# Two hybrid-encoder layers on one core: the linear attention's values leave the PE transposes and travel through device memory, the output projection starts in two banks of another pool, and a pool closes two tiles later

## The chip, the cores and the metric

The kernel runs on one core of a Trainium2 chip. The metric is the device time of one execution in microseconds, as the median of several runs; smaller is better. Before the change it is 2322.85 us (three runs, 2322.03 to 2323.6).

## What is computed

Two encoder layers run over 272 positions (16 learned meta tokens and 256 grid tokens) of width 2048, in float32. Each layer makes one combined projection, runs two groups of heads beside each other on its columns, joins them by an output projection, and follows with two post-LN steps and a squared-ReLU MLP:

```python
proj = jnp.einsum('bld,dp->blp', h, w_in)
gq, gk, gv, gr, glr, nq, nk, nv = jnp.split(proj, points, axis=-1)
y_gla = _gla_mixer(gq, gk, gv, gr, glr, gla_w_up, gla_b_up, gla_norm_w)   # 4 heads, dk 128, dv 256
y_na = _na_mixer(nq, nk, nv, na_rel_bias)                                 # 16 heads of 64
mix = jnp.einsum('blm,md->bld', jnp.concatenate([y_gla, y_na], axis=-1), w_out)
h = _layer_norm(DEEPNORM_ALPHA * h + mix, ln1_w, ln1_b)
ff = jnp.einsum('blf,fd->bld', jnp.square(jax.nn.relu(jnp.einsum('bld,df->blf', h, w_ff1))), w_ff2)
return _layer_norm(DEEPNORM_ALPHA * h + ff, ln2_w, ln2_b)
```

The GLA heads (gated linear attention, both directions) need each position's values v as rows: positions on the partitions, the 256 value channels along them. Their output is normalised per head by `rsqrt(mean(o*o))`, so a sum over 256 channels is needed per position. The NA heads (neighbourhood attention) are softmaxes over a window of keys plus the 16 meta tokens; in the first layer the meta tokens' own softmax is computed too. The last layer needs only the 256 grid tokens behind its attention.

## The kernel before

**Matmuls.** Every float32 product is made of three: each operand is split into a high part (rounded to the matmul's type, fp32r) and a low part, the rest, and high x high, high x low and low x high are summed in PSUM. Weights stream in by SP's DMA as `raw` tiles of 128 x 1024. ACT casts each to `wh` (L218) and DVE subtracts to get `wl` (L219); the rings of `raw`, `wh` and `wl` are three deep, and the weight tile behind the one in use is asked for ahead. One weight tile feeds 24 matmuls of 128 x 272.

**Two ways through a projection.** `by_m` (L317) makes one output tile (128 columns of the projection by 272 positions) at a time, in one PSUM bank of the pool `pm` (tiles called "mm", four banks), over the whole depth of 2048. `by_k` (L279) makes four output tiles at once, each in a bank of its own, two blocks of the depth at a time: it can begin while later parts of its input are still being made. The pool `pb` (tiles called "bg", four banks, `bank()`) holds what the background work needs.

**Background.** Attention, gates and normalisation are Python generators in two queues, `fg` and `bg`. Between weight tiles `pump` (L127) steps them, so that their instructions fall among the projection's matmuls. Every engine runs its own instructions in the order in which it got them, so an instruction that waits holds back all behind it on its engine.

**A layer** (L353 on). The columns of the projection come in this order. First k and the values of heads 0 and 1, by `by_k` (in layer 0 eight tiles, four of them in banks of `pb`; in layer 1 the values alone). Then the values of heads 2 and 3 by `by_m`, four tiles; then q. Meanwhile the gates are made (L470 to L494: a low-rank product, its copy `lrt`, the cast `lr` on ACT, and matmuls that read `lr`). Then the gate r and the 24 tiles of the NA heads' q, k and v, in six groups of four; beside these the four GLA heads run as `gla_head` in `bg`. Before the last group (`g == 5`) all of `bg` is forced out, the pool of the GLA heads is closed (`gctx.close`) and that of the layer norm opened (`ln_open`). Then `by_k` makes the first four tiles of the output projection `w_out` (L413), reading `self.y`, which the last NA pair is still filling: `mixed` waits block by block for what is done. Its other twelve tiles go by `by_m`.

**Values.** The projection leaves v with channels on the partitions. `ev_v` (L503) copies a result tile to `ft` on ACT; when a head's two tiles are there, `v_rows` (L510) turns them with six PE transposes (L518: two 128 x 128 and one of 16 columns for each tile) into two "mm" banks, from which ACT casts the high part `V` (L339), DVE subtracts the low part (L340, into `vlow`, which lies in tiles of `y` that are not used yet), and `stack` (L345, L346) places the 16 meta rows in `VS`.

**Other lines of the change.** In `gla_head`, L721 squares the two halves of a head's output on ACT (`grs`, `gtn`), L725 adds them on DVE, L339 and L340 split the sum (`sp`), and `mean` (L976) sums it over the channels by matmuls with a matrix of constants (L983). In an NA pair, `softmax` (L752) runs on the scores `ns` and, in layer 0, on the meta rows' scores `nms`; its reciprocals are on DVE (L757), the multiplies by them (L760) on POOL for `ns` and `npr` and on DVE for `nms`. DVE then turns `ns` and `npr` in squares of 32 x 32 (L799, L800) and ACT's queue sends the result to device memory as `hop` (L819), whence SP's queue fetches it in four pieces (L826); that puts keys on the partitions. PE turns the pair's values and, in layer 0, `nms` (L805, L806, L808) into a "bg" bank.

Of the kernel before, what the change touches and what calls it, by code (L numbers as in the profile page):

```python
# [14 lines left out]
P = 128  # L15
# [24 lines left out]
PITCH = 288  # L40
WIDE = 1280
# [17 lines left out]
class Trunk:  # L59
# [219 lines left out]
    def by_k(self, acts, n, before, wide=False):  # L279

        ps = [self.pm.tile([P, 512], F32, name="mm", tag="mm") for _ in range(4)]
# [3 lines left out]
        for k in range(0, nk, 2):  # L285
# [4 lines left out]
            for g in range(0, len(ps), 4):  # L290
# [62 lines left out]
    def layer(self, l):  # L353
# [4 lines left out]
        with ExitStack() as actx:  # L358
# [8 lines left out]
            self.V = a.tile([P, 2 * GH, 2, P], F32R, name="V", tag="V")  # L367
# [3 lines left out]
            self.y, self.gate, self.done, self.vt = [None] * DC, {}, set(), []  # L371
# [7 lines left out]
            with ExitStack() as ectx:  # L379
# [11 lines left out]
                self.credit, self.alone = 0, True  # L391
                self.by_m(self.x, [L] * 4, lambda m, ps: self.ev_v(4 + m, ps), pump=(1, 1, True))
# [3 lines left out]
            with ExitStack() as gctx:  # L396
# [106 lines left out]
    def ev_v(self, c, ps):  # L503
        vt = self.ep.tile([P, L], F32, name="ft", tag="ft", bufs=4)
        self.nc.scalar.copy(vt, ps)
# [4 lines left out]
    def v_rows(self, h, vt):  # L510

        nc = self.nc
        yield True
        pt = self.spare(2)
        for i in range(3):
            n = P if i < 2 else NM
            for e in range(2):
                nc.tensor.transpose(pt[e][:n, i * P:i * P + P], vt[e][:, i * P:i * P + n], self.ident)  # L518
        for e in range(2):
            self.split(pt[e][:, :T], self.V[:, 2 * h + e].rearrange("p i c -> p (i c)"), self.vlow[h][:, e * T:e * T + T])  # L520
# [761 lines left out]
```

## Time and profile before

| | |
|---|---|
| median of three runs | 2322.85 us |
| the profiled execution | 2323.91 us, its span 2322.1 us |
| clock granted to TensorE | 0.999 |
| PE busy | 2304.2 us (99%), 18420 matmuls |
| DVE busy | 1526.4 us (66%) |
| ACT busy | 1223.0 us (53%) |
| POOL busy | 155.4 us (7%) |
| DMA | 431.65 MB, mean 186 GB/s |

The profile's page gives, for one execution, the busy time of each engine; the chain of waits (the work that ended last, followed back through whatever released it); groups of instructions by line; and the DMA queues. A row of a timeline shows the start, the duration, the engine, the line, the operation, what it writes and reads ("out<-in"), the shape, how many such instructions follow each other, and in square brackets how long the engine stood idle ahead of it and for whom. Lines are those of the kernel before unless said otherwise.

### The profile page before, as it was taken

What the parts mean: (1) busy time and instruction counts of PE and PEld (TensorE: products, weight loads), DVE (VectorE), ACT (ScalarE), POOL (GpSimd) and SP (SyncE); (2) the same over time, 40 slices, a digit from 0 to 9 for tenths busy, and PEclk for the clock granted to TensorE, in tenths of its full rate; (3) what the DMA queues carried; (4) which work ended last, traced back from release to release, by engine and by line L of the source; (5) the groups of instructions that cost most, each with busy time, mean ns of one, the idle gap of its engine ahead of it and who ended that gap; (6) DMA issues with size and microseconds to landing.
All of it is one profiled execution on the core that took longest, in us unless ns stands there. A gap on an engine that the chain in (4) does not pass through costs nothing.

```text
span 2322.1 us, 45272 instructions
## 1 busy us (share of the span) xinstructions
PE 2304.2 (99%) x18420; PEld 2188.9 (94%) x18420; DVE 1526.4 (66%) x2408; ACT 1223.0 (53%) x2096; POOL 155.4 (7%) x232
## 2 busy tenths in 40 slices
PE   9999999999999999999999999999999999999998
PEld 9999999999999999999999899889988888888888
DVE  5588878875544455547576788688866555666655
ACT  5666655564433344444456766655654334555443
POOL 0023210100000000000020122200100000000000
PEclk9999999999999999999999999999999999999999
DMA  8556666565555556665655556665666666667664
GB/s 259 155 164 184 199 189 177 173 181 181 182 181 178 179 181 182 180 179 178 182 173 173 173 175 209 195 187 181 198 191 196 194 191 193 192 196 218 195 195 150
DMA packets 129824, 431.65 MB, mean 186 GB/s; under 512 B 14792, under 2 KB 23496, under 8 KB 129616
## 3 DMA queue, kind: packets, MB, share of 16 engines
q1 hardware_dynamic: 127024, 421.95, 59.9%
q10 hardware_dynamic: 2592, 6.82, 0.8%
q8 instruction: 144, 2.36, 0.4%
q14 instruction: 64, 0.52, 0.1%
HBM read 420.32 MB, written 8.39 MB: 185 GB/s over the span
## 4 chain that ended last, share of the span: by engine, by line
PE 91%; DVE 5%; ACT 2%; issue 1%; DMA 1%; POOL 0%; DVEq 0%; ACTq 0%; SPq 0%
PE mm L253 53%; PE mm L265 29%; PE mm L304 4%; PE mm L314 2%; DVE wl L219 1%; PE bg L304 1%; ACT wh L218 1%; ACT ns L756 0%; DVE S L615 0%; PE bg L851 0%; PE bg L470 0%; PE bg L629 0%; DVE acc L1085 0%; POOL dec L617 0%; DMA raw<-in_wff 0%
## 5 line engine op out<-in xcount | busy, mean ns | idle before, releaser
L219 DVE TENSOR_TENSOR wl<-raw,wh 128x1024 fp32r<-128x1024 f32 (+1 forms) x770 | 935.9, 1223 | 621.8 <-ACT wh L218 518.5
L218 ACT CAST wh<-raw 128x1024 fp32r<-128x1024 f32 (+1 forms) x770 | 804.7, 1047 | 755.8 <-PE mm L253 352.6
L253 PE MATMUL mm<-x,wh 128*128 128x272 f32 (+3 forms) x4544 | 806.8, 294 | 0.0
L253 PEld LDWEIGHTS mm<-x,wh 128*128 128x128 f32 x4544 | 648.0, 188 | 15.5 <-issue 0.8
L253 PE MATMUL mm<-x,wl 128*128 128x272 f32 (+3 forms) x2432 | 520.6, 285 | 2.9 <-DVE wl L219 2.9
L253 PEld LDWEIGHTS mm<-x,wl 128*128 128x128 f32 x2432 | 391.4, 188 | 3.4 <-DVE wl L219 3.4
L253 PE MATMUL mm<-y,wh 128*128 128x272 f32 (+1 forms) x1440 | 235.0, 285 | 0.0
L253 PEld LDWEIGHTS mm<-y,wh 128*128 128x128 f32 x1440 | 199.7, 188 | 0.1
L265 PE MATMUL mm<-x,wh 128*128 128x512 f32 x832 | 193.8, 390 | 0.0
L265 PEld LDWEIGHTS mm<-x,wh 128*128 128x128 f32 x832 | 154.3, 188 | 31.0
L253 PE MATMUL mm<-u,wh 128*128 128x272 f32 (+1 forms) x1056 | 172.1, 285 | 0.0
L265 PE MATMUL mm<-y,wh 128*128 128x512 f32 x688 | 162.3, 389 | 0.0
L265 PEld LDWEIGHTS mm<-y,wh 128*128 128x128 f32 x688 | 128.7, 188 | 26.8 <-issue 0.4
L253 PE MATMUL mm<-y,wl 128*128 128x272 f32 (+1 forms) x720 | 146.5, 284 | 0.0
L253 PEld LDWEIGHTS mm<-u,wh 128*128 128x128 f32 x1056 | 146.3, 188 | 0.0
L265 PE MATMUL mm<-u,wh 128*128 128x512 f32 x496 | 118.3, 391 | 0.0
L253 PEld LDWEIGHTS mm<-y,wl 128*128 128x128 f32 x720 | 112.5, 188 | 0.0
L265 PEld LDWEIGHTS mm<-u,wh 128*128 128x128 f32 x496 | 90.9, 188 | 17.6
L253 PE MATMUL mm<-u,wl 128*128 128x272 f32 (+1 forms) x528 | 107.4, 284 | 0.0
L265 PEld LDWEIGHTS mm<-x,wl 128*128 128x128 f32 x832 | 98.5, 188 | 2.1
L265 PE MATMUL mm<-x,wl 128*128 128x256 f32 x832 | 99.0, 276 | 0.0
L265 PEld LDWEIGHTS mm<-y,wl 128*128 128x128 f32 x688 | 84.3, 188 | 2.8
(275 smaller groups left out, 2285.0 us busy)
## 6 DMA issues: line engine op xcount, KB each, us to landing
raw<-in_wff SPq DMA_DIRECT2D x512, 512.0 KB, 3.6
raw<-in_win SPq DMA_DIRECT2D x190, 512.0 KB, 4.2
raw<-in_wout SPq DMA_DIRECT2D x64, 512.0 KB, 3.9
hop<-nt ACTq DMA_DIRECT2D x16, 384.0 KB, 2.3
np<-hop SPq DMA_DIRECT2D x64, 96.0 KB, 4.1
nb<-in_nab SPq DMA_DIRECT2D x16, 352.0 KB, 4.4
xraw<-in_xT SPq DMA_DIRECT2D x7, 272.0 KB, 5.8
out<-out SPq DMA_DIRECT2D x5, 256.0 KB, 3.1
```

Source lines behind the costliest of these rows:

```text
L218: self.nc.scalar.copy(h, r)
L219: self.wl = self.nc.vector.tensor_tensor(lo, r, h.bitcast(F32), ALU.subtract).ins
L253: mm(o, lhsT=self.block(w, j), rhs=rhs, start=first and not i, stop=last and i == len(TURNS[once]) - 1)
L265: self.nc.tensor.matmul(o, lhsT=self.block(both[j // 8][low], j % 8), rhs=rhs, start=first and not i + j, stop=bool(last and i and j == 15 ...
L304: self.nc.tensor.matmul(ps[g + m][:, :n], lhsT=self.block(parts[p][0], 4 * j + m if first else 2 * m + j), rhs=acts[k + j][parts[p][1]][:, ...
L314: self.nc.tensor.matmul(o, lhsT=self.block(both[low], i), rhs=rhs, start=not low and k + i % 2 == 0, stop=k == DC - 2 and i % 2 == 1 and n ...
```

## The change

Five edits:

1. `by_k` for `w_out` takes its first two result tiles from `pb` and only the last two from `pm` (`ends=True`), and orders the matmuls of the first weight tile by result tile too, the "bg" tiles first.
2. The last NA group is run as two halves of two tiles. Forcing out `bg`, closing the GLA pool and opening the layer norm's come between the halves, two tiles later than before.
3. The values: `ev_v` copies to a tile `ft` padded to 128 x 288 (DVE zeroes the last 16 columns) and turns it in 32 x 32 squares on DVE. A generator `v_flow` then moves each head: `w` writes the turned tile to device memory (`vhop`, 295 KB), `r` reads it back in eight pieces of 32 partitions (32 KB each, straight into `vlow`) and one of 16 (`vm`, the meta rows), all on POOL's DMA queue; `s` casts `V` from what landed (ACT, 128 x 512), subtracts the low part in place (DVE) and stacks the meta rows. The columns of v in the weights are permuted beforehand to fit. The PE transposes and their two "mm" banks go.
4. The sum of the two squared halves (L725) moves from DVE to POOL.
5. The multiply of the meta rows' softmax (L760 for `nms`) moves from DVE to POOL.

```diff
-    def by_k(self, acts, n, before, wide=False):
-        ps = [self.pm.tile([P, 512], F32, name="mm", tag="mm") for _ in range(4)]
+    def by_k(self, acts, n, before, wide=False, ends=False):
+        tile = lambda n: [self.pm.tile([P, 512], F32, name="mm", tag="mm") for _ in range(n)]
+        ps = [self.bank(), self.bank()] + tile(2) if ends else tile(4)
...
-                    order.sort(key=lambda o: (k and o[2], o[1] // 2, o[2]))
+                    order.sort(key=lambda o: ((k or ends) and o[2], o[1] // 2, o[2]))
...
                 for g in range(6):
-                    if g == 5:
-                        while self.bg:
-                            self.step(self.bg, 1)
-                        gctx.close()
-                        self.ln_open()
                     ns = [n if (4 * g + m) % 3 == 0 else L for m in range(4)]
-                    self.by_m(self.x, ns, lambda m, ps: self.ev_na(4 * g + m, ps), pump=(1, GLA_NA, True))
+                    for at in ((0, 2), (2, 4)) if g == 5 else ((0, 4),):
+                        if at == (2, 4):
+                            while self.bg:
+                                self.step(self.bg, 1)
+                            gctx.close()
+                            self.ln_open()
+                        self.by_m(self.x, ns[slice(*at)], lambda m, ps: self.ev_na(4 * g + at[0] + m, ps), pump=(1, GLA_NA, True))
             self.alone = False
-            ps = self.by_k(self.y, n, self.mixed)
+            ps = self.by_k(self.y, n, self.mixed, ends=True)
...
     def ev_v(self, c, ps):
-        vt = self.ep.tile([P, L], F32, name="ft", tag="ft", bufs=4)
-        self.nc.scalar.copy(vt, ps)
-        self.vt.append(vt)
-        if c % 2:
-            (self.fg if c > 3 else self.bg).append(self.v_rows(c // 2, self.vt[-2:]))
+        e = c % 2
+        if not e:
+            self.vt = self.ep.tile([P, VR, 2, 32], F32, name="vt", tag="vt", bufs=4)
+        t = self.ep.tile([P, VR * 32], F32, name="ft", tag="ft", bufs=2)
+        self.nc.scalar.copy(t[:, :L], ps)
+        self.nc.vector.memset(t[:, L:], 0.0)
+        self.nc.vector.transpose(self.vt[:, :, e, :], t)
+        if e:
+            self.vts.append(self.vt)
...
+    def v_flow(self):
+        nc, ep = self.nc, self.ep
+        hops, metas = {}, {}
+        def w(h):
+            hops[h] = self.hp.tile([P, VR, 64], F32, name="vhop", tag="vhop", bufs=4)
+            nc.gpsimd.dma_start(hops[h], self.vts[h].rearrange("p j e c -> p j (e c)"))
+        def r(h):
+            raw = self.vlow[h][:, :2 * T].bitcast(F32).rearrange("p (i a c) -> p i a c", i=2, a=4)
+            metas[h] = ep.tile([NM, GDV], F32, name="vm", tag="vm", bufs=4)
+            at = hops[h].rearrange("(a k) j c -> k j a c", a=4)
+            for j in range(VR - 1):
+                nc.gpsimd.dma_start(raw[j % 4 * 32:j % 4 * 32 + 32, j // 4], at[:, j])
+            nc.gpsimd.dma_start(metas[h].rearrange("p (a c) -> p a c", a=4), at[:NM, VR - 1])
+        def s(h):
+            low, to = self.vlow[h][:, :2 * T], self.VS[:, h * GDV:h * GDV + GDV]
+            high = self.V[:, h].rearrange("p i c -> p (i c)")
+            nc.scalar.copy(high, low.bitcast(F32))
+            nc.vector.tensor_tensor(low, low.bitcast(F32), high.bitcast(F32), ALU.subtract)
+            self.stack(metas[h], to, NM, (0, 32), 64)
+        for f, h in ((w, 0), (w, 1), (r, 0), (w, 2), (r, 1), (s, 0), (r, 2), (w, 3), (s, 1), (r, 3), (s, 2), (s, 3)):
+            while len(self.vts) <= h:
+                yield
+            f(h)
+            yield
...
-        nc.vector.tensor_tensor(rs, rs, tn, ALU.add)
+        nc.gpsimd.tensor_tensor(rs, rs, tn, ALU.add)
...
-            self.softmax(sm, mt, 2, ((sm, sm),), nc.vector)
+            self.softmax(sm, mt, 2, ((sm, sm),), nc.gpsimd)
```

The rows below are instructions in the order in which each engine gets them: the line, the operation, what it writes and reads, the shape, and "x2" where two alike follow each other. Names are those of the tiles; the numbers behind a name only tell tiles apart. The lines of the changed kernel stand a little further down than those of before (L218 and L219 become L219 and L220, L304 becomes L306).

**ACT, the value stage of layer 0**, from the last casts ahead of the gates on. Before:

```order
L218 CAST wh<-raw 128x1024 x2
L475 COPY lrt<-bg 32x272
L505 COPY ft<-mm 128x272
L339 CAST V<-mm 128x256
L345 CAST lr<-lrt 32x272 x2
L345 CAST VS<-mm 16x128 x2
L339 CAST V<-mm 128x256
L345 CAST VS<-mm 16x128 x2
L218 CAST wh<-raw 128x1024
```

and now:

```order
L219 CAST wh<-raw 128x1024 x2
L512 COPY ft<-mm 128x272
L479 COPY lrt<-bg 32x272
L347 CAST lr<-lrt 32x272 x2
L538 CAST V<-y_91 128x512
L347 CAST VS<-vm 16x256 x2
L219 CAST wh<-raw 128x1024
```

The cast of `V` reads `y_91`, the tile of `y` that holds head 0's `vlow`, and the casts of `VS` read `vm`: both are written by DMA now, and the next weight tile's cast stands behind them. In the same place of layer 1 the gates' casts stand behind them too:

```order
L219 CAST wh<-raw 128x1024
L538 CAST V<-y_14761 128x512
L347 CAST VS<-vm 16x256 x2
L479 COPY lrt<-bg 32x272
L347 CAST lr<-lrt 32x272 x2
L219 CAST wh<-raw 128x1024
```

Before, that place of layer 1 read `lrt`, `ft`, `V`, `lr`, with nothing that a DMA brings.

**POOL, the value stage of layer 0**, all of it new; `y_91` to `y_94` are the four heads' `vlow`:

```order
L525 DMA vhop<-vt 128x576 x2
L532 DMA y_91<-vhop 32x4x64 x8
L533 DMA vm<-vhop 16x4x64
L532 DMA y_92<-vhop 32x4x64 x8
L533 DMA vm<-vhop 16x4x64
L525 DMA vhop<-vt 128x576
L532 DMA y_93<-vhop 32x4x64 x8
L533 DMA vm<-vhop 16x4x64
L525 DMA vhop<-vt 128x576
L532 DMA y_94<-vhop 32x4x64 x8
L533 DMA vm<-vhop 16x4x64
```

Head 1's reads stand behind all nine of head 0; a read must wait until its `vhop` has landed.

**PE, the start of `w_out` in layer 0**, behind the last NA pair's scores (L782 before, L807 now; they write the last two "mm" tiles ahead of it). Before:

```order
L782 MATMUL mm<-nk,nq 64x48 x2
L304 MATMUL mm<-y_1488,wh 128x272 x2
L304 MATMUL mm<-y_1566,wh 128x272 x2
L304 MATMUL mm<-y_1488,wh 128x272 x2
L304 MATMUL mm<-y_1566,wh 128x272 x2
L304 MATMUL mm<-y_1488,wl 128x272
L304 MATMUL mm<-y_1566,wl 128x272
```

and now:

```order
L807 MATMUL mm<-nk,nq 64x48 x2
L306 MATMUL bg<-y_1504,wh 128x272 x2
L306 MATMUL bg<-y_1582,wh 128x272 x2
L306 MATMUL bg<-y_1504,wl 128x272
L306 MATMUL bg<-y_1582,wl 128x272
L306 MATMUL bg<-y_1504,wh 128x272 x2
L306 MATMUL bg<-y_1582,wh 128x272 x2
L306 MATMUL bg<-y_1504,wl 128x272
L306 MATMUL bg<-y_1582,wl 128x272
L306 MATMUL mm<-y_1504,wh 128x272 x2
```

Twelve matmuls of the two "bg" tiles now stand ahead of the first that writes an "mm" tile; before, all four tiles were "mm".

More of the change, by code (lines that the diff above doesn't have):

```diff
@@ L40 @@
 PITCH = 288
+VR = 9
 WIDE = 1280
@@ L366, in layer @@
             self.decay = [t(f"dec{h}", [P, 2, L]) for h in range(GH)]
-            self.V = a.tile([P, 2 * GH, 2, P], F32R, name="V", tag="V")
+            self.V = a.tile([P, GH, 2, GDV], F32R, name="V", tag="V")
             self.vlow = [self.pair(self.yp, "y", 12 + h).both.rearrange("p a c -> p (a c)") for h in range(GH)]
@@ L370, in layer @@
             nc.gpsimd.memset(self.VS.bitcast(F32), 0.0)
-            self.y, self.gate, self.done, self.vt = [None] * DC, {}, set(), []
+            self.y, self.gate, self.done, self.vts = [None] * DC, {}, set(), []
             if l:
@@ L391, in layer @@
                 self.credit, self.alone = 0, True
+                self.bg.append(self.v_flow())
                 self.by_m(self.x, [L] * 4, lambda m, ps: self.ev_v(4 + m, ps), pump=(1, 1, True))
@@ L503, in ev_v @@
     def ev_v(self, c, ps):
-        vt = self.ep.tile([P, L], F32, name="ft", tag="ft", bufs=4)
-        self.nc.scalar.copy(vt, ps)
-        self.vt.append(vt)
-        if c % 2:
-            (self.fg if c > 3 else self.bg).append(self.v_rows(c // 2, self.vt[-2:]))
[L510 to L520, printed above, removed]
-            self.stack(pt[e][:NM, T:T + P], self.VS[:, h * GDV + e * P:h * GDV + e * P + P], NM, (0, 32), 64)
+        e = c % 2
@@ L714, in gla_head @@
             for i in range(2):
-                v, vl = self.V[:, 2 * h + e, i, :], self.vlow[h][:, e * T + i * P:e * T + i * P + P]
+                c = slice(e * P, e * P + P)
+                v, vl = self.V[:, h, i, c], self.vlow[h][:, i * T:i * T + T][:, c]
                 nc.tensor.matmul(o, lhsT=v, rhs=high[:, i, :], start=not i, stop=False)
```

1 line of the change is left out of this document (added).

## The prediction

> **What bounds the kernel.** I read the page first, then PE's waits summed over the span.
>
> ```profile
> PE 2304.2 (99%) x18420; PEld 2188.9 (94%) x18420; DVE 1526.4 (66%) x2408; ACT 1223.0 (53%) x2096; POOL 155.4 (7%) x232
> PE bg L983 <- ACT sp L339: 3.3, 3, 1.2
> PE mm L314 <- DVE nr L541: 0.9, 1, 0.9
> PE mm L304 <- DVE nr L541: 0.8, 1, 0.8
> PE mm L304 <- DVE nms L789: 0.8, 1, 0.8
> PE bg L808 <- DVE nms L760: 0.7, 1, 0.7
> ```
>
> (Waits: who waits for whom, total us, times, longest.) PE is busy 99% of the span. So a change can win only by giving PE less to do or by removing one of these short waits; everything else is hidden until it makes PE wait. In the stage where layer 0 makes its values, a window (length, then busy us of PE, PEld, DVE, ACT, POOL) shows no slack on PE and much elsewhere:
>
> ```profile
> 50.00:104.00 54.00, 54.00 (x443) 53.60 (x442) 31.45 (x47) 37.29 (x76) 0.32 (x1) 1.00 0.52 158
> ```
>
> **Term 1: the PE transposes go, -5.3 us.** Eight groups of six (four heads, two layers):
>
> ```profile
> L518 PE MATMUL mm<-ident,ft 128*128 128x128 f32 x32 | 4.8, 272 | 0.0
> 71.79 0.65 PE L253 MATMUL mm<-x,wh 128*128 128x272 f32 x4
> 72.28 0.41 PE L253 MATMUL mm<-x,wl 128*128 128x272 f32 x2
> 72.53 0.42 PE L488 MATMUL bg<-lr,up 98*128 98x272 f32 x2
> 72.78 0.82 PE L518 MATMUL mm<-ident,ft 128*128 128x128 f32 x6
> 73.36 0.75 PE L253 MATMUL mm<-x,wh 128*128 128x272 f32 x4
> 73.94 0.41 PE L253 MATMUL mm<-x,wl 128*128 128x272 f32 x2
> ```
>
> Matmuls overlap, so I price by starts, not by the 272 ns: a group starts at 72.78 and the next matmul at 73.36, 0.58 us; the four `wh` matmuls behind it take 0.58 to the next start where the four from 71.79 to 72.28 took 0.49. 0.67 x 8 = 5.3 us, with 4.6 (0.58 alone) as the other bound. What replaces them on DVE and ACT costs PE nothing as such: DVE turns 128x512 in 0.705 us and 128x256 in 0.406,
>
> ```profile
> L799 DVE STREAM_TRANSPOSE nt<-ns 128x512 f32<-128x512 f32 x16 | 11.3, 705 | 7.5 <-POOL ns L760 7.5
> L800 DVE STREAM_TRANSPOSE nt<-npr 128x256 f32<-128x256 f32 x16 | 6.5, 406 | 0.0
> ```
>
> so 128x288 is about 0.44. Sixteen of these, sixteen small zeroings (0.1 estimated), eight subtractions of 128x512 (0.68) and eight stacks (0.42) make 17.5 us over both layers against 10.9 for the subtractions and stacks before (sixteen of 0.42 and of 0.28): 3.3 us more per layer, in a stage where DVE has 22 us idle (54.00 - 31.45). ACT gets about 3 us less.
>
> **Term 2: the start of `w_out`, -1.7 us.** Timeline of PE in layer 0, and the same place in layer 1 (last row):
>
> ```profile
> 335.38 0.77 PE L304 MATMUL mm<-y,wh 128*128 128x272 f32 x4 [0.83 <-DVE nr L541]
> 337.48 0.74 PE L304 MATMUL mm<-y,wh 128*128 128x272 f32 x4 [0.83 <-DVE nms L789]
> 343.48 0.30 PE L808 MATMUL bg<-ident,nms 128*128 128x128 f32 x1 [0.70 <-DVE nms L760]
> 1514.10 1.96 PE L314 MATMUL mm<-y,wh 128*128 128x512 f32 x6 [0.89 <-DVE nr L541]
> ```
>
> PE stands until DVE has read the "mm" banks of the last tiles. With two "bg" tiles first it has twelve matmuls, 1.5 us at 123 ns, to do meanwhile, longer than 0.83 and 0.89: these three waits, 2.55 us, go. But the fourth, on `nms`, gets a new owner and PE gets there earlier:
>
> ```profile
> 342.19 1.04 POOL L760 TENSOR_TENSOR ns<-ns,nst 128x512 f32<-128x512 f32 x1 [6.74 <-DVE nst L757]
> 343.18 0.52 POOL L760 TENSOR_TENSOR npr<-ns,nst 128x192 f32<-128x192 f32 x1
> 342.56 0.78 DVE L760 TENSOR_TENSOR nms<-nms,mst 16x96 f32<-16x96 f32 x1
> ```
>
> On POOL `nms` stands behind `ns` and `npr`: they end at 343.7 where DVE ended `nms` at 343.34, so `nms` is ready some 0.7 later relative to the scores, while PE arrives 1.7 earlier and the scores' own chain moves up by less, since half of it was never behind PE. I take a wait of 1.55 instead of 0.70: 2.55 - 0.85 = 1.7 won. Bounds: 3.25 (all four waits go) and 0.2 (PE merely waits at `nms` instead). The other full-size NA pairs of layer 0 meet the same longer wait only where PE is close behind; I add +0.4 for one. Two banks fewer for background work during `w_out` (the last two pairs' outputs need two and the value turn one) could add up to half a microsecond; taken as nothing because their matmuls lie some twenty matmuls, 2.5 us, apart.
>
> **Term 3: the mean of the GLA heads, -3.0 us.**
>
> ```profile
> 302.48 0.41 ACT L721 ACTIVATE gtn<-bg 128x272 f32<-128x272 f32 x1
> 304.66 0.43 DVE L725 TENSOR_TENSOR grs<-grs,gtn 128x272 f32<-128x272 f32 x1
> 305.59 0.87 PE L983 MATMUL bg<-sp,onesr 128*128 128x272 f32 x2 [1.13 <-ACT sp L339]
> 1485.08 0.84 PE L983 MATMUL bg<-sp,onesr 128*128 128x256 f32 x2 [0.97 <-ACT sp L339]
> L617 POOL TENSOR_TENSOR dec<-dec 128x272 f32<-128x272 f32 x8 | 6.0, 754 | 126.4 <-DVE S L615 126.4
> ```
>
> The squares are ready at 302.89, the sum starts on DVE only at 304.66. POOL adds such tiles in 0.75 us (last row) and is idle, so it ends near 303.7 against 305.09: 1.4 earlier, more than the wait of 1.13. For the other two, both in layer 1, I reckon the same with their shorter queues on DVE (1.0 and 0.9 earlier), and the later close gives the last head's mean more matmuls to hide behind. Of 3.3 I take 3.0; bounds 0 and 3.3.
>
> **Term 4: the values' way through memory, +3.0 us.** This is the open price: no DMA issued by POOL is in the trace. Let c be POOL's time to issue one, and l the time from issue to landing.
>
> ```profile
> hop<-nt ACTq DMA_DIRECT2D x16, 384.0 KB, 2.3
> np<-hop SPq DMA_DIRECT2D x64, 96.0 KB, 4.1
> 333.11 1.75 SPq L826 DMA_DIRECT2D np<-hop  x4
> 50.80 0.86 ACT L505 COPY ft<-bg 128x272 f32<-128x272 f32 x2
> 51.78 0.68 DVE L340 TENSOR_TENSOR ws<-gw,ws 128x512 fp32r<-128x512 f32 x1
> 63.74 0.86 ACT L345 CAST lr<-lrt 32x272 fp32r<-32x272 f32 x2
> 72.21 0.66 ACT L490 ACTIVATE gt<-gt 128x544 f32<-128x544 f32 x1
> 1236.17 0.95 ACT L505 COPY ft<-mm 128x272 f32<-128x272 f32 x3
> 1246.03 1.05 ACT L218 CAST wh<-raw 128x1024 fp32r<-128x1024 f32 x1 [1.88 <-PE mm L253]
> ```
>
> l lies between 2.3 and 4.1; I take 3. SP issues one in 1.75/4 = 0.44 us; POOL is slower than DVE at the same add by 754/422 = 1.8, which gives 0.8, and I take c = 0.9, with 0.44 and 1.05 (the large multiply above) as bounds. A head's write must land (l), then eight reads are issued one behind the other (seven c after the first) and the last lands (l): 2l + 7c = 12.3 us after the write; head 1's come nine issues later. In layer 0 the first two copies end at 51.7; DVE has `ws` until 52.46, then two turns and zeroings (1.1), so the write goes at 53.5: head 0 is there at 65.8 and head 1 at 73.9, where ACT reaches their casts at about 64.3 (behind the `lr` casts of 63.74, less the value copies that go) and 73.8 (behind the gate's L490 of 72.21 and the work ahead of it that the first stop delays). In layer 1 the copies end at 1237.1, the two turns and zeroings take 1.1, the write goes at 1238.4 and head 0 lands at 1250.7. ACT comes to its cast at 1247.1 and stands there; behind it are the meta casts (their piece lands c later), `lrt` and `lr`, so `lr` is ready near 1253.8, where PE wants it at about 1253.0: 0.8 us lost. The next weight tile's cast stands behind `lr` and its subtraction on DVE another 1.2 behind that, worth 0.8 more. In layer 0 two such stops of at most 1.5 behind casts that come two weight tiles (5.9 us) ahead of need: I allow 1.4. Together 3.0. With the low bounds (c 0.44, l 2.3) nothing is lost; with the high ones (1.05 and 4.1) the same working gives 3.5 + 1.5 + 3 in layer 0 and 4 + 3 in layer 1, 15 us.
>
> The Trainium skill, "DMA: Bandwidth & Descriptors", section "Anatomy of one DMA — SWDGE (gpsimd) path", fits a GpSimd transfer at 2.0 us plus its bytes over 436e3; by that, as an estimate, a 32 KB piece takes 2.1 us and the loss of layer 1 would vanish, the sum coming out some 2 us lower. No run here shows it yet.
>
> **Sum.** The profiled span is 2322.1. -5.3 - 1.7 + 0.4 - 3.0 + 3.0 = -6.6: span 2315.5. That execution took 2323.91 in all, 1.81 around its span; the median of the runs shown, 2322.85, lies 0.75 above the span, which gives 2316.2 for the median after; I say 2316.
>
> **Rivals.** *Slower: POOL's issues are held up by DVE.* The trace has one row in which a tiny POOL instruction met a DVE pass over a weight tile:
>
> ```profile
> 277.08 1.41 POOL L617 TENSOR_TENSOR dec<-dec 128x8 f32<-128x8 f32 x1 [1.21 <-DVE S L615]
> 277.20 1.21 DVE L219 TENSOR_TENSOR wl<-raw,wh 128x1024 fp32r<-128x1024 f32 x1
> 279.03 0.33 POOL L617 TENSOR_TENSOR dec<-dec 128x4 f32<-128x4 f32 x1 [0.54 <-DVE S L615]
> ```
>
> The first took 1.41 us, the next, half its size, 0.33: the first shared its time with `wl` on DVE, which ended at 278.41, as it nearly did (278.49). DVE is busy 58% of the value stage (31.45 of 54). If every issue that meets such a pass is held, c becomes about 0.9 + 0.58 x 0.6 = 1.25, head 1 lands at 79.5 in layer 0 and head 0 at 1253.2 in layer 1; ACT stands 5.7 us at head 1's cast (79.5 - 73.8), 2.8 beyond the one weight tile (2.9 us) that is cast ahead; heads 2 and 3, each nine issues later, meet much the same, some 9.5 lost in the layer. In layer 1 `lr` comes at 1256.3 instead of 1253.0 and two later heads add as in layer 0, some 8. 17.5 instead of 3.0: 2330. It decides once the losses exceed ten. Against it: both are tensor adds that read the same memory; an issue need not.
>
> The Trainium skill, "SBUF — State Buffer", section "SBUF: two separate sides", speaks against the change here: it says that a DVE pass in a two-port mode keeps GpSimd from writing its descriptors, so that such a transfer waits. By it the time would be that of this rival.
>
> *No change: the gains are given back.* c 1.05 and l 3.5 lose about 8 in the value stages, or the waits at `w_out` and the means come back on POOL (terms 2 and 3 at their low bounds, together 4.5 less): 2320 to 2323. For it: PE is full, so every late cast counts; against it: ACT has 17 us idle in that stage.
>
> *The change does what it says with no stall at all*: terms 1 to 3 whole and term 4 nothing, 2322.85 - 11.9 = 2311.
>
> *The `w_out` edit does nothing*: PE reaches `nms` early and waits there for what it saved; only layer 1's 0.89 and little else are won. 0.8 slower than forecast, inside its range.
>
> **Chances and range.** Forecast and its neighbours 0.42 (own range 2312 to 2319), no stall at all 0.12, gains given back 0.22, POOL held up 0.24. What a measurement of this kernel can tell from no change is 0.2%, 4.6 us, so under 2318.2 is faster and over 2327.5 slower: faster 0.54, same 0.22, slower 0.24. The range takes in both the no-stall case and most of the losses: 2310 to 2330.
>
> **What would show it.** Term 1: no PE transposes of `ft` and 48 matmuls fewer on PE. Term 2: PE's rows of `w_out` without the waits on `nr` and on the scores, a wait on POOL's `nms` of 1.5 in their place. Term 3: no wait of L983 on `sp` over 0.3. Term 4: the eight reads of a head 0.9 apart on POOL's queue, landing 3 us behind their issue; ACT's cast of `V` idle ahead of it for a DMA, and PE waiting for `wl` or `lr` by 3 us in all. Wrong it would be if the reads stand over 1.1 us apart (then the losses grow by some 1 us for each 0.05), or if PE waits at a place that none of the terms names.

## The result, and the profile after

The changed kernel takes 2320.16 us (median of 22 runs, 2317.35 to 2323.89) against 2323.15 us for the kernel before (22 runs, 2321.36 to 2326.37). The ratio is 0.9987, with an interval of 0.9981 to 0.9993: 3.0 us faster, where 6.9 were forecast. The profiled execution took 2318.52 us, its span is 2316.7 us, 5.4 less than the span of before. So there are two gaps to explain: from 6.6 forecast to 5.4 in the profiled span, and from there to 3.0 in the median.

The page's first line and the rows of PE's timeline that show a stop (in brackets: idle time ahead of the row, and whom it waited for). Left out are one of 0.40 at 38.52 on `wl`, and two that before has alike (1.22 at the start, 0.67 at 1213.86):

```profile
PE 2298.5 (99%) x18372; PEld 2183.3 (94%) x18372; DVE 1524.5 (66%) x2408; ACT 1221.6 (53%) x2072; POOL 204.1 (9%) x328
103.29 0.75 PE L254 MATMUL mm<-x,wh 128*128 128x272 f32 x4 [0.46 <-ACT wh L219]
104.55 0.52 PE L254 MATMUL mm<-x,wl 128*128 128x272 f32 x2 [0.51 <-DVE wl L220]
217.34 0.33 PE L833 MATMUL bg<-ident,nms 128*128 128x128 f32 x1 [0.34 <-POOL nms L785]
340.86 0.33 PE L833 MATMUL bg<-ident,nms 128*128 128x128 f32 x1 [2.50 <-POOL nms L785]
1254.43 0.49 PE L492 MATMUL bg<-lr,up 98*128 98x272 f32 x2 [2.45 <-DVE ft L513]
1327.82 0.84 PE L1008 MATMUL bg<-sp,onesr 128*128 128x256 f32 x2 [0.57 <-ACT sp L341]
1455.50 0.52 PE L254 MATMUL mm<-x,wl 128*128 128x272 f32 x2 [2.11 <-DVE wl L220]
1509.24 0.73 PE L316 MATMUL mm<-y,wh 128*128 128x512 f32 x2 [0.26 <-DVE nr L565]
1517.69 0.87 PE L876 MATMUL bg<-np,v 64*64 64x128 f32 x20 [0.55 <-DVE v L837]
```

PE has 48 matmuls fewer (18420 to 18372) and 5.7 us less busy time: the transposes are gone. Its idle time is as long as before (2316.7 - 2298.5 = 18.2 us, 17.9 before), but in other places. The waits on `nr` and on the scores (0.83, 0.83, 0.89) and on `sp` (3.32 in all), 5.9 us, shrank to 0.26 and 0.57; in their place stand a stop of 2.50 us on `nms`, 0.70 before, and one of 2.45 in layer 1. For the second the row names DVE's `ft` (L513), a small zeroing that starts while PE already waits; what PE needs is `lr`, as ACT's timeline shows (PE's last matmul for the gates started at 1248.7, so what `lrt` copies was ready from about 1249.0 on):

```profile
1244.82 1.05 ACT L219 CAST wh<-raw 128x1024 fp32r<-128x1024 f32 x1 [1.60 <-PE mm L254]
1250.61 0.62 ACT L538 CAST V<-y 128x512 fp32r<-128x512 f32 x1 [4.73 <-DMA y<-vhop]
1251.69 0.82 ACT L347 CAST VS<-vm 16x256 fp32r<-16x256 f32 x2 [0.46 <-DMA vm<-vhop]
1252.53 0.38 ACT L479 COPY lrt<-bg 32x272 f32<-32x272 f32 x1
1253.40 0.86 ACT L347 CAST lr<-lrt 32x272 fp32r<-32x272 f32 x2 [0.49 <-DVE lrt L480]
```

ACT stands 4.73 us until head 0's pieces have landed; `lrt`, which could have gone some 3.5 us earlier, and `lr` are behind. POOL's own rows give the two prices that no row of before had, and the landings of the queues beside them:

```profile
1237.50 0.62 POOL L525 DMA_DIRECT2D vhop<-vt  x1 [6.80 <-DVE ft L513]
1242.18 4.44 POOL L532 DMA_DIRECT2D y<-vhop  x8 [1.41 <-DMA vhop<-vt]
vhop<-vt POOLq DMA_DIRECT2D x8, 288.0 KB, 4.1
y<-vhop POOLq DMA_DIRECT2D x64, 32.0 KB, 3.9
hop<-nt ACTq DMA_DIRECT2D x16, 384.0 KB, 3.2
np<-hop SPq DMA_DIRECT2D x64, 96.0 KB, 5.3
```

An issue takes POOL 4.44 / 8 = 0.55 us, not 0.9, and a piece lands after 3.9 us, not 3. DVE ran two subtractions over whole weight tiles at 1243.66 and 1245.90 while these eight issues went out evenly, and all 64 reads of the profile took 0.55 to 0.57 us to issue: the rival in which DVE holds them up is refuted. The Trainium skill's page "SBUF — State Buffer", section "Who interferes with whom", says as much of this kind of pass: a `tensor_tensor` with both inputs in SBUF contends with GpSimd's reads only; here the trace agrees.

### The profile page after: what moved, and what is told of

Same layout as the page of the kernel before. It is cut to its first block, busy times and chain, and to the rows that moved or that the text cites. A ratio compares the mean times of both kernels' runs of the same rounds, so it can differ in the third digit from the quotient of the medians.

```text
span 2316.7 us, 45339 instructions
## 1 busy us (share of the span) xinstructions
PE 2298.5 (99%) x18372; PEld 2183.3 (94%) x18372; DVE 1524.5 (66%) x2408; ACT 1221.6 (53%) x2072; POOL 204.1 (9%) x328
## 4 chain that ended last, share of the span: by engine, by line
PE 88%; DVE 4%; DMA 3%; issue 2%; ACT 2%; POOL 1%; SPq 0%; DVEq 0%; ACTq 0%; POOLq 0%
PE mm L254 51%; PE mm L266 30%; PE mm L306 2%; DVE wl L220 1%; PE mm L316 1%; DMA raw<-in_win 1%; ACT wh L219 1%; DMA vhop<-vt 1%; PE bg L306 1%; DMA y<-vhop 1%; PE bg L876 0%; PE bg L316 0%; PE bg L653 0%; POOL y L532 0%; DMA vm<-vhop 0%
## 5 line engine op out<-in xcount | busy, mean ns | idle before, releaser
L220 DVE TENSOR_TENSOR wl<-raw,wh 128x1024 fp32r<-128x1024 f32 (+1 forms) x770 | 935.9, 1223 | 623.7 <-ACT wh L219 515.6
L219 ACT CAST wh<-raw 128x1024 fp32r<-128x1024 f32 (+1 forms) x770 | 804.9, 1047 | 750.7 <-PE mm L254 344.6
```

Source lines behind the costliest of these rows:

```text
L219: self.nc.scalar.copy(h, r)
L220: self.wl = self.nc.vector.tensor_tensor(lo, r, h.bitcast(F32), ALU.subtract).ins
```

## The experiments

All kernels below compute the whole reference. Ratios are to the kernel before, measured on the same chip. "The clock's part" is (1 - mean granted clock of the runs) x 2320 us; it is explained with the first four kernels. It holds a share that costs nothing: in all 14 profiles the last 0.7 to 3.2 us of the span, behind PE's last matmul, are at half clock, worth 0.4 to 1.6 us of the part there. So the parts are to be compared with each other, not read as losses. The runs of before in the first table come from the three sessions with experiments, those of the whole change from a session of their own.

### The parts of the change, and two repairs

`v_only` has edit 3 alone; `no_v` has the four others. `nms_dve` undoes edit 5. `lr_first` forces one order: `self.lr` is the second cast of `lr` (`stack`, not shown, returns it), and what is traced inside `issue_after` comes behind it on its engine, ACT.

```diff
# nms_dve
-            self.softmax(sm, mt, 2, ((sm, sm),), nc.gpsimd)
+            self.softmax(sm, mt, 2, ((sm, sm),), nc.vector)
# lr_first
-        self.stack(t, lr, 32, (0, 64), 32)
+        self.lr = self.stack(t, lr, 32, (0, 64), 32)
...
+            with self.tc.issue_after(self.lr):
+                nc.scalar.copy(high, low.bitcast(F32))
+                nc.vector.tensor_tensor(low, low.bitcast(F32), high.bitcast(F32), ALU.subtract)
+                self.stack(metas[h], to, NM, (0, 32), 64)
```

> The kernel before with edit 3 alone (values through device memory). Theory (the terms add): PE loses the transposes, 5.3 us, and gets the waits that the changed kernel's trace shows in the two value stages, 2.45 on lr, 0.46 on wh and 0.51 on wl, 3.4 in all: 1.9 us faster than before, ratio 0.9992; PE waits 2.4 for lr in layer 1, and the waits of before at the output projection (0.83, 0.83, 0.70, 0.89) and at the GLA means (1.13, 1.22, 0.97) stand as they were. Rival A (the software DMA queue costs beyond its own waits): same as before or slower in the median, with longer landings of the other transfers (hop near 3.2 us instead of 2.3, np near 5.3 instead of 4.1) although they lie in other stages. Rival B (POOL's issues are held by DVE): issues over 1 us each.

> The kernel before with edits 1, 2, 4 and 5, without edit 3. Theory: +0.1 at the first output projection (2.36 of waits go, one of 2.5 on the meta softmax comes), +0.3 at an earlier NA pair, -0.1 at the second projection, -2.75 at the GLA means, -0.6 from a wait on wl at 278: about 3.0 us faster than before, ratio 0.9987, and no change in the landing times of hop (2.3) and np (4.1). Rival A (edit 3 costs as much as it saves): as fast in the median as the whole change, or faster. Rival C (the pool edits only shift work that is made up later): no gain, ratio 1.000.

> The whole change with the multiply of the meta softmax back on DVE (edit 5 undone). Theory: the wait of 2.50 us at the first output projection is POOL's order, nms behind ns and npr; on DVE it falls to 0.5 to 1.3, and the 0.34 at an earlier pair goes: 1.5 to 2.3 us faster than the whole change, ratio to before near 0.9979. Rival: PE comes 1.7 us earlier and the scores' own chain is late, so a wait of 2 us or more stays on the same row, whoever multiplies; under 0.5 us gained.

> The whole change with one order forced: on ACT each head's V and VS casts stand behind the casts of lr (moves only head 0's of layer 1). Theory: the 2.45 us that PE waits for lr in layer 1 go, since lr no longer stands behind casts that wait for the DMA of POOL's queue; 2.4 us faster than the whole change, ratio to before near 0.9977. Rival: the casts of V and VS, now later, hold the next weight tile's cast, and PE waits for wh or wl instead by 1 us or more.

| kernel | runs | median | ratio | interval | mean clock | the clock's part | mean without it |
|---|---|---|---|---|---|---|---|
| before | 86 | 2323.36 | | | 0.99902 | 2.3 | 2321.0 |
| the whole change | 22 | 2320.16 | 0.9987 | 0.9981 to 0.9993 | 0.99845 | 3.6 | 2316.8 |
| v_only | 11 | 2325.37 | 1.0013 | 1.0004 to 1.0022 | 0.99836 | 3.8 | 2322.0 |
| no_v | 11 | 2319.28 | 0.9983 | 0.9974 to 0.9992 | 0.99882 | 2.7 | 2316.4 |
| nms_dve | 11 | 2320.35 | 0.9988 | 0.9979 to 0.9997 | 0.99845 | 3.6 | 2316.5 |
| lr_first | 6 | 2316.00 | 0.9969 | 0.9958 to 0.9981 | 0.99900 | 2.3 | 2313.8 |

**no_v** is as fast as the whole change: rival A of its expectation. What edit 3 saves on PE it costs again. **v_only** is slower than before in the median, though its profiled span (2320.7) is 1.4 shorter, and its theory is missed. The profiled execution is the fastest of its eleven. In it PE stops 1.60 us for `lr`, but the waits on `nr` at the two output projections, which the theory left as they were, are 1.48 and 1.28 us for 0.83 and 0.89 before. What made the other ten longer is open: the clock's part is 1.5 above before's, and 1.0 more lies outside it.

**lr_first** finds the cost. On ACT nothing moved but head 0's `V` and `VS`, behind `lr`:

```profile
1248.11 0.38 ACT L480 COPY lrt<-bg 32x272 f32<-32x272 f32 x1 [3.18 <-PE bg L475]
1248.98 0.86 ACT L347 CAST lr<-lrt 32x272 fp32r<-32x272 f32 x2 [0.49 <-DVE lrt L481]
1249.87 0.62 ACT L540 CAST V<-y 128x512 fp32r<-128x512 f32 x1
1251.12 0.82 ACT L347 CAST VS<-vm 16x256 fp32r<-16x256 f32 x2 [0.63 <-DMA vm<-vhop]
```

`lr` is ready 4.4 us earlier (1249.84 for 1254.26), PE's stop of 2.45 is gone, and of the other stops the means' grows most (0.57 to 1.12). The profiled span falls by 2.1 us (2316.7 to 2314.6). The median of its six runs lies 4.2 us under that of the change, measured in another session: more than the stop.

**nms_dve**: the rival was right, the wait stays. The start of the scores, the end of the `nms` multiply and PE's stop, first of the change, then of `nms_dve`:

```profile
330.65 0.81 PE L803 MATMUL mm<-nk,nq 64*64 64x176 f32 x16
340.47 0.34 POOL L785 TENSOR_TENSOR nms<-nms,mst 16x96 f32<-16x96 f32 x1
```

```profile
331.94 0.81 PE L803 MATMUL mm<-nk,nq 64*64 64x176 f32 x16
341.36 0.67 DVE L785 TENSOR_TENSOR nms<-nms,mst 16x96 f32<-16x96 f32 x1
342.17 0.30 PE L833 MATMUL bg<-ident,nms 128*128 128x128 f32 x1 [2.13 <-ACT wh L219]
```

From the scores to `nms` it takes 10.2 us with POOL (340.81 - 330.65), 10.1 with DVE (342.03 - 331.94). In this place POOL does the multiply in 0.34 us and DVE in 0.67, so its place behind `ns` and `npr` in POOL's row costs what it wins. DVE is not the slower one as such: in the layer's seven other pairs it takes 0.20 to 0.25 us and POOL 0.34 to 0.54; only here does it start while POOL is multiplying `ns`, and it ends 0.11 us behind that (342.03 behind 341.92; 343.34 behind 343.23 in the kernel before). That it waits for POOL there fits the rows; no run takes it away. PE is there 7.7 us after the scores (340.86 - 2.50 - 330.65). So PE waits for the softmax chain itself, which nobody shortened, and every stop taken away ahead of it only brings PE there sooner.

**The clock.** Why did `lr_first`'s runs win more than the stop? Windows of four microseconds (busy us of PE, PEld, DVE, ACT, POOL, then the granted clock) around the same two stops, of the profiled change and of a second profile of the same kernel (`after_again`, below):

```profile
338.00:342.00 4.00, 1.50 (x12) 1.28 (x12) 2.93 (x8) 2.77 (x12) 1.80 (x3) 1.00 0.46 131
342.00:346.00 4.00, 4.00 (x47) 3.75 (x45) 1.63 (x7) 1.23 (x3) 0.00 (x0) 0.57 0.63 229
1252.00:1256.00 4.00, 1.57 (x12) 1.60 (x13) 1.57 (x4) 3.40 (x9) 1.07 (x3) 1.00 0.15 29
1256.00:1260.00 4.00, 4.00 (x34) 4.00 (x33) 2.89 (x7) 3.94 (x9) 0.56 (x1) 1.00 0.49 186
```

```profile
338.00:342.00 4.00, 1.31 (x9) 1.10 (x8) 2.93 (x8) 2.98 (x13) 1.80 (x3) 0.94 0.45 135
342.00:346.00 4.00, 4.00 (x32) 3.85 (x34) 1.87 (x6) 0.62 (x4) 0.00 (x0) 0.64 0.71 229
1252.00:1256.00 4.00, 1.52 (x13) 1.33 (x12) 1.01 (x4) 3.15 (x7) 1.70 (x4) 1.00 0.21 41
1256.00:1260.00 4.00, 4.00 (x22) 4.00 (x22) 3.31 (x6) 2.80 (x6) 0.56 (x1) 0.57 0.46 130
```

Behind a stop PE is 100% busy at a granted clock of 0.57 to 0.64: it runs at half speed for some 3.4 us, and 4 x (1 - 0.57) = 1.7 us are lost. In the first profile that follows the stop at 340 and not the one at 1254, in the second both, with stops of the same length (2.45 and 2.48 us). Over the 14 profiles of this study 24 stops were of 2.0 to 2.9 us, and 15 were followed by such a stretch; of 10 stops between 1.25 and 2.0 us, 3 were; of the shorter ones, none.

It is not chance which stop is followed. The clock records of the traces lie on a grid of 3.413 us: every stretch begins a whole number of 3.413 us behind the trace's first record, and lasts one such step. Windows cut on that grid, around the two stops in the profiled change and then around the one in layer 1 in `after_again`:

```profile
338.66:342.08 3.42, 1.22 (x10) 1.23 (x11) 2.35 (x6) 2.11 (x8) 1.80 (x3) 1.00 0.55 158
1250.02:1253.43 3.41, 1.96 (x16) 1.74 (x15) 0.43 (x1) 1.83 (x5) 3.05 (x6) 1.00 0.48 126
1253.43:1256.84 3.41, 2.41 (x19) 2.44 (x20) 1.98 (x4) 3.31 (x7) 0.00 (x0) 1.00 0.05 8
```

```profile
1252.85:1256.26 3.41, 1.28 (x10) 1.31 (x11) 1.27 (x4) 2.82 (x7) 0.85 (x2) 1.00 0.18 31
```

The stop of 2.45 us lay across two windows, with 1.45 and 1.00 us of idle time, and no stretch followed; the one of 2.48 put 2.13 into one window, and a stretch followed, as behind the 2.20 idle at 338.66. In the 14 profiles 17 windows held 1.77 us of PE's idle time or more, and each was followed by a stretch; of some 9,400 others one was (1.30 us idle, in `v_only` at 1509). The nine stops over 2 us without a stretch had at most 1.75 us in either window. What differs between executions of one kernel is where the grid lies under its stops.

Before has one stop over 2 us (2.32 at 1457), the change has three. By these counts two more stops cost 2 x 15/24 x 1.7 = 2.1 us on average, on top of their length; the mean clocks in the table give 3.6 - 2.3 = 1.3 (0.5 to 2.2 by resampling the runs).

### The repair again, with one edit undone at a time

Four kernels on `lr_first`: the meta rows' softmax traced ahead of the big one, and edits 1, 4 and 2 undone.

```diff
# lr_nms_first
-        self.softmax(s, st, 4, ...)
-        yield
         if self.full:
             ...
             self.softmax(sm, mt, 2, ((sm, sm),), nc.gpsimd)
         yield
+        self.softmax(s, st, 4, ...)
+        yield
# lr_ends_off
-            ps = self.by_k(self.y, n, self.mixed, ends=True)
+            ps = self.by_k(self.y, n, self.mixed)
# lr_grs_dve
-        nc.gpsimd.tensor_tensor(rs, rs, tn, ALU.add)
+        nc.vector.tensor_tensor(rs, rs, tn, ALU.add)
# lr_close_early
-                        if at == (2, 4):
+                        if at == (0, 2):
```

> lr_first with the meta rows' softmax traced ahead of the big one (reduction, exponentials, reciprocal and multiply of nms before those of ns, on DVE, ACT and POOL alike). Theory: what PE waits for at the start of the first output projection is the length of the softmax chain, some 10.1 us from the scores to nms whoever multiplies, while PE comes after 7.7; with nms first it is ready some 2 us earlier, the stop of 2.7 falls under 0.7, and with it goes the stretch of about 3.4 us at half the granted clock that follows such a stop in some executions (1.7 us): 2.0 to 3.7 us faster than lr_first (2316.0), near 2313. Rival: ns and with it hop and np come 1 us later, and PE waits for them instead (rows of the pair's output) by 1 us or more: no gain.

> lr_first with edit 1 undone (all four first tiles of the output projection in mm). Theory: edit 1 only gathers three stops (0.83, 0.83, near 0.9) into one of 2.7 in layer 0 and saves 0.7 in layer 1: within 1.0 us of lr_first (2316.0) either way, and no half-clock stretch at 340 to 350 us since no stop there is over 1.5. Rival (the prediction's term): 1.7 us slower, 2317.7.

> lr_first with edit 4 undone (the sum of the squares on DVE). Theory: the waits of L1010 (L983 before) on sp come back at 0.8 to 1.2 each in two or three places: 1.5 to 2.5 us slower than lr_first, near 2318. Rival: the later close hides the last head's mean anyway; one wait comes back, under 0.8 us.

> lr_first with edit 2 undone (the close before the whole last group). Theory: the sum on POOL has taken most of the waits; the last heads' mean waits 0 to 0.5 us in each layer, and a wait of 0.6 on wl at 278 us comes back: 0.5 to 1.5 us slower than lr_first, near 2317. Rival: the close alone carries the gain of the means, 2 us or more slower.

| kernel | runs | median | ratio | interval | the clock's part | mean without it |
|---|---|---|---|---|---|---|
| lr_nms_first | 6 | 2317.66 | 0.9975 | 0.9963 to 0.9986 | 1.2 | 2317.0 |
| lr_ends_off | 11 | 2320.42 | 0.9983 | 0.9974 to 0.9991 | 4.0 | 2316.1 |
| lr_grs_dve | 11 | 2319.37 | 0.9983 | 0.9974 to 0.9992 | 4.4 | 2315.1 |
| lr_close_early | 11 | 2318.72 | 0.9974 | 0.9965 to 0.9983 | 3.2 | 2315.3 |

**lr_nms_first** does what it was made for: the stop on `nms` is 0.20 us, and its profile has no half-clock stretch ahead of the program's last ten microseconds. The median gains nothing on `lr_first`, and the profile little: its span of 2313.9 has no stretch, and that of `lr_first`, 2314.6, has one, worth 1.7. Seven new stops of 0.25 to 0.81 us stand elsewhere, among them one for `np`: the rival, with the gain given back in more places than it named. Six runs from 2315.48 to 2323.13 settle no more than that.

**lr_ends_off** shows what edit 1 is worth. Its stops at the two output projections:

```profile
334.83 0.77 PE L306 MATMUL mm<-y,wh 128*128 128x272 f32 x4 [1.81 <-DVE nr L567]
336.93 1.24 PE L306 MATMUL mm<-y,wh 128*128 128x272 f32 x4 [0.82 <-DVE nms L816]
344.49 0.33 PE L835 MATMUL bg<-ident,nms 128*128 128x128 f32 x1 [0.81 <-POOL nms L787]
1511.15 1.26 PE L316 MATMUL mm<-y,wh 128*128 128x512 f32 x3 [1.58 <-DVE nr L567]
```

3.44 us in layer 0 against 2.70 with the edit, 1.58 against 0.71 in layer 1 (0.16 and 0.55): 1.6 us, close to the prediction's 1.7 and not to the theory's "within 1.0". But the wait on `nr` is longer here than in the kernel before (1.81 for 0.83, 1.58 for 0.89), so part of what the edit saves is what the rest of the change brought: `v_only`, which has edit 3 alone, shows the same two waits (1.48 and 1.28). A half-clock stretch did stand at 336: two stops, 1.81 and 0.82, lie 2.1 us apart and together put 2.14 us of idle time into one window of the grid.

**lr_grs_dve and lr_close_early** divide term 3. With both edits the means wait 1.12 us in one place (`lr_first`); with the sum back on DVE 1.77 in one place; with the early close 0.16, 0.56 and 0.39, together 1.11; with neither 3.32 (before). So the sum alone takes two thirds of the 3.32, the later close alone under half, and together they take what the sum takes, or some more: with both, the means wait 0.56 to 1.16 us in the eight other profiles that have them. The theory for the sum (1.5 to 2.5 slower) is missed in the profile, its rival (under 0.8) hit: 0.65 of stops. The medians, 2.4 and 1.8 above the median of all 17 runs of `lr_first`, hold more of the clock: without its part these kernels lie 0.7 and 0.9 above that one (2314.4). For the close the theory's 0.5 to 1.5 fits, but its wait on `wl` at 278 did not come back.

### The change and the repair side by side, and two more

`after_again` and `lr_first_again` are the whole change and `lr_first`, unedited. `lr_last_first` has the meta softmax first for the last pair only. `v_lr` is `v_only` with the order of `lr_first`.

> The whole change, unedited, a second profile of it. Theory: its stops at the first output projection (2.5), on lr in layer 1 (1.6 to 2.9 in the three profiles that have it, set by when the DMA of POOL's queue lands) and on wl near 1455 (2.1) stand again, and each is followed in some executions by 3.4 us at half clock, 1.72 us lost: zero to three such stretches in this profile, median 2319 to 2321. Rival: the profile that the prediction was compared with is typical and the median is raised by something else; then this one shows no more than one such stretch, and its time outside stops and stretches is 1 us or more longer than before's.

> lr_first, unedited, beside the whole change on the same chip. Theory: 2.5 for the stop and up to 1.7 for the half-clock stretch behind it: 2.5 to 4.2 us faster than the whole change, and a smaller spread of the runs. Rival: the first session's 2316.0 was luck; within 1.5 us of the whole change.

> lr_first with the meta softmax ahead of the big one for the last NA pair alone. Theory: the stop of 2.7 at the first output projection falls under 0.5, nothing else moves, and the half-clock stretch there is gone: 2.5 us faster than lr_first in the profile without counting stretches, 2.5 to 4 in the median, near 2313. Rival: the pair's big softmax, its transfers and its output come 1 us later and PE waits for them within the same projection; under 1 us gained.

> The kernel before with edit 3 alone and lr ahead of V and VS on ACT. Theory: what made edit 3 alone slower than before (2325.4 against 2323.3) is the stop on lr with the stretch behind it; without it the transposes' 5.3 us less about 1.0 for short stops near 103 us remain: 3 to 5 us faster than before, near 2319. Rival: the DMA traffic of POOL's queue costs elsewhere; then no faster than before, as edit 3 alone.

| kernel | runs | median | ratio | interval | the clock's part | mean without it |
|---|---|---|---|---|---|---|
| after_again | 11 | 2319.41 | 0.9985 | 0.9976 to 0.9994 | 3.4 | 2315.9 |
| lr_first_again | 11 | 2317.63 | 0.9978 | 0.9969 to 0.9986 | 3.0 | 2314.7 |
| lr_last_first | 8 | 2317.27 | 0.9975 | 0.9965 to 0.9985 | 2.0 | 2315.3 |
| v_lr | 11 | 2323.49 | 1.0005 | 0.9996 to 1.0014 | 4.0 | 2319.7 |

**after_again** has the stops of the first profile (2.69, 2.48, 2.27 for 2.50, 2.45, 2.11) and three half-clock stretches for one. Its span is 2320.4 for 2316.7: of the 3.7 us two stretches are 3.4 and the stops 0.4. The same kernel, the same stops, and the difference between two executions is the clock, by where its grid lay.

**lr_first_again** is 1.8 us faster than the change beside it, where 2.5 to 4.2 were expected; the intervals overlap. Over all runs the medians are 2319.98 (33 of the change) and 2316.92 (17 of `lr_first`), 3.1 apart. Its range, 2315.44 to 2321.16, is no narrower than before's: the narrow range of the first six was chance. It is the fastest version that stood two measurements, and beats the kernel before in both; that it beats the change rests on the two sessions together.

**lr_last_first**: the rival; the stop did not fall under 0.5. PE waits less for `nms` and more for what now comes later:

```profile
338.69 0.33 PE L840 MATMUL bg<-ident,nms 128*128 128x128 f32 x1 [1.31 <-POOL nms L787]
350.04 1.52 PE L883 MATMUL bg<-np,v 64*64 64x128 f32 x18 [1.00 <-DMA np<-hop]
```

2.68 became 1.31 + 1.00, and the median gains 0.4.

**v_lr** misses its theory. Its profiled span is 2319.1, 3.0 under before's with one half-clock stretch each, but its median is not under before's. The rows of its waits:

```profile
PE mm L306 <- DVE nr L567: 1.5, 1, 1.5
PE mm L316 <- DVE nr L567: 1.3, 1, 1.3
PE mm L254 <- ACT wh L219: 0.8, 1, 0.8
```

The waits on `nr` grew from 0.83 and 0.89 as in `lr_ends_off`; with 0.75 and 0.50 near 103 us that is 2.3 us given back. In the means 1.3 us are won outside the clock and 1.7 lost in it. That the longer stops on `nr` bring the stretches is not shown: its one profile has a stretch behind the stop on `wl` at 1452 alone, and of the four such stops in `v_only` and `v_lr` one was followed. Edit 3 with the repaired order is worth something beside the other edits (`lr_first` against `no_v`, the same session: 3.3 us in the medians, 2.6 without the clock) and nothing in the median by itself; what edit 1 does for the waits on `nr` is part of that, the rest is open.

## Why the prediction came out as it did

**Direction and range held, the size did not.** 2320.16 lies in 2310 to 2330 and above the likeliest case's own 2312 to 2319; the change is real, but under the 0.2% that was named as the least that can be told, so the case "gains given back" (0.22) is nearest to it.

| term | forecast | in the profile |
|---|---|---|
| 1, transposes | -5.3 | -5.7 (PE's busy time in all) |
| 2, start of `w_out` | -1.7 | +0.1 (3.25 to 3.31) |
| 2, an earlier pair | +0.4 | +0.3 |
| 3, means | -3.0 | -2.75 (3.32 to 0.57) |
| 4, values through memory | +3.0 | +3.4 (2.45, 0.46, 0.51) |
| other stops (278, 1457, start) | none | -0.7 |
| sum | -6.6 | -5.4 (span -5.4) |
| half-clock stretches | none | 0 (one in each of these two profiles), +1.3 in the mean of the runs |

**Term 1** held within 0.4: counting starts, not durations. **Term 3** was right in size, and in cause: it credited the sum on POOL first and the later close second, and undone one at a time the sum is the larger part. Its sign, no wait over 0.3, failed at one place (0.57).

**Term 2 is the step that failed, in size and in the reason it named.** It took the wait on `nms` to grow from 0.70 to 1.55 because POOL does it last. It grew to 2.50, as the rival "the `w_out` edit does nothing" had it for layer 0, and POOL is not why: DVE in POOL's place left 2.13. The chain from the scores takes 10.1 to 10.2 us; PE's way there became 2.1 us shorter (9.8 after the scores before: 343.48 - 0.70, from scores that start at 332.95; 7.7 now). The prediction had PE 1.7 earlier and `nms` 0.7 later behind the scores, and let all but 0.85 of that be hidden; PE came 2.1 earlier, `nms` 0.2 earlier (10.4 us behind the scores before), and nearly the whole difference became waiting. In layer 1 the wait on `nr` fell to 0.26, but one of 0.55 came behind it (1517.69). Every profile with edit 1 has it and none without, so edit 1 brings it. It may be the half microsecond from two banks fewer that the prediction named and took as nothing; that the banks are the cause is not shown.

```profile
332.95 0.81 PE L778 MATMUL mm<-nk,nq 64*64 64x176 f32 x16
```

**Term 4 was right in sum by luck, with both prices off in opposite ways**: 0.55 for 0.9 us an issue, 3.9 for 3 us to land. Head 0's pieces were there at 1250.6, as forecast (1250.7), and `lr` at 1254.3 (1253.8). The loss was 2.45 and not 0.8 + 0.8 because PE wanted `lr` at 1251.98, not 1253.0: that time was read off the kernel before, and by then the changed program was 1.2 us ahead and had no transposes between. The gates' matmuls (first and last start), before and after:

```profile
L470 PE MATMUL bg<-x,ws x64: 282/287/295, 58.4 to 1249.9; 128*64 128x272 f32 x32, 128*32 128x272 f32 x32
```

```profile
L474 PE MATMUL bg<-x,ws x64: 282/287/290, 58.7 to 1248.7; 128*64 128x272 f32 x32, 128*32 128x272 f32 x32
```

In layer 0 0.97 was lost for 1.4. The rival with DVE holding POOL's issues was refuted.

**The missing step is the price of a stop.** The prediction counted each by its length. Three stops over 2 us, where before had one, bring stretches at half the granted clock in some executions; in the means of the runs that is 1.3 us, and without it the change is 4.2 us faster than before (2321.0 to 2316.8). The profiled difference of 5.4 was kinder than the median's 3.0 because the one profiled execution lay 0.8 above its median (2323.91 against 2323.15) and the other 1.6 under it (2318.52 against 2320.16); the 1.2 us between 5.4 and 4.2 are not assigned. Edit 1 gathers short stops into a long one in layer 0. Three stops of 0.8 us would have the length of one of 2.4 without that risk, as long as no window of the grid holds two or three of them; in `lr_ends_off` two fell into one, and a stretch followed.

## What to carry to other kernels

When work moves from the bound engine to a path of transfers, look on every engine at what stands behind the first instruction that waits for them: here one order on ACT, `V` ahead of `lr`, cost 2.45 us, nearly half of what the removed transposes saved, and turning it round made the change worth 6 us instead of 3 over all runs (5 instead of 3.5 where both ran in one session, with overlapping intervals). Price a due time in the changed program's own time, since an engine relieved earlier arrives earlier, and a wait that is not shortened at its source grows by that much. On a kernel that keeps PE 99% busy, count a stop of 2 to 3 us as its length plus about one more microsecond (15/24 x 1.7), and prefer short ones that lie more than 3.4 us apart.

## What the runs showed of the hardware that was not expected

**Half clock after short stops.** Of 24 stops of PE between 2.0 and 2.9 us, 15 were followed by some 3.4 us at a granted clock of half, 1.7 us lost each; the same stop in the same kernel was followed by it in one execution and not in another. What decides is the idle time inside one window of a grid of 3.413 us: 1.77 us or more in 17 windows, a stretch behind each; at most 1.75 in the others, a stretch behind one. The Trainium skill's page "TensorE: Matmul & The Clock Gate", Part 1, tells of an activity window of 3.4 us that runs freely, and names idle gaps over about 3.4 us as what throttles; that the onset depends on the window's phase agrees with these rows, the length does not: 1.77 us were enough, and in one case a window with 1.30.

**POOL's DMA queue**: 0.55 us an issue and 3.9 us to landing for 32 KB. The Trainium skill's page "DMA: Bandwidth & Descriptors", section "Anatomy of one DMA — SWDGE (gpsimd) path", gives an estimate of 2.1 us for that size by its fit; the measurement decides.

**Other queues' landings.** `hop`, sent by ACT's queue in stages in which POOL sends nothing, landed after 2.3 us in before and 2.5 in `no_v`, and after 3.0 to 3.3 in eleven of the twelve profiles of kernels with edit 3 (4.0 in `lr_nms_first`). In `no_v` and in `v_lr`:

```profile
hop<-nt ACTq DMA_DIRECT2D x16, 384.0 KB, 2.5
```

```profile
hop<-nt ACTq DMA_DIRECT2D x16, 384.0 KB, 3.3
```

Why is open; no experiment here tells.
